# Norm tiles moved to another pool, a cross-attention head delayed by one unit, a quieter schedule in the second layer, and whole output rows at the end

## The chip, the core and the metric

The kernel is one program on one core of a Trainium2 chip. The metric is the time of one execution in microseconds (us) as the device measures it. Three timed executions of the kernel before took 946.2, 946.23 and 946.56 us, with a median of 946.23 us. A profiled execution of its own took 946.38 us.

The engines are named as in the profile: PE is TensorE (PEld its weight loads), DVE is VectorE, ACT is ScalarE, POOL is GpSimd and SP is SyncE, which here only issues DMAs.

## The reference

One step of a two-layer streaming encoder. There are 256 prompt frames and 32 sample frames (288 columns in all), 1024 features, 256 memory tokens and a feed-forward width of 2816. Cut to what matters:

```python
for layer in range(2):
    if layer == 0:   # 8 heads of chunk attention + 8 heads of stick-breaking attention
        x = x + merge_heads(chunk_attn(...), stick_break(...)) @ w_out_ab
    else:            # 16 heads of softmax attention with a forget bias
        q, k, v, log_f = proj_c(rmsnorm(x, g_mix), w_in_c, b_f)
        s = q @ k.T * 64 ** -0.5 + (cum_q - cum_k);  s = where(k_pos <= q_pos, s, -1e30)
        x = x + merge_heads(softmax(s) @ v) @ w_out_c
    mk, mv = memory_kv(mem, g_mem, w_xk, w_xv)               # 4 heads of 256
    x = x + (softmax(q4 @ mk.T / 16) @ mv) @ w_xo             # q4 = rmsnorm(x, g_xattn) @ w_xq
    x = x + (silu(h @ w_gate) * (h @ w_up)) @ w_down          # h = rmsnorm(x, g_ffn)
y = rmsnorm(x, g_final)                                        # rows are frames
```

`rmsnorm(x, g)` is `x * rsqrt(mean(x * x) + 1e-6) * g`. The keys and values are outputs too. All of it is float32.

## The kernel before

The residual `x` lies transposed in SBUF: eight blocks of 128 features by 288 columns. Every large product is done in a split form: an operand is cut into a rounded part (`hi`, `hh`, `oh`, `qh`) and the rest (`lo`, `hl`, `ol`, `ql`), and three matmuls (`mm3`, L193) add up to one product.

**Units.** The weights come in some 250 units. A unit is one 512 KB DMA of a 128x1024 tile `st` (issued by SP), a cast `hi` on ACT (L162), a subtraction `lo` on DVE (L163) and 24 matmuls into a PSUM bank. The tag `pj` has four banks; in the profile the matmuls are `pj` (projections and feed-forward), `op` (output projections), `mv` (memory values) and `dn` (down projection). All the small work, scores, transposes, softmax sums, uses another four banks of the tag `at` in turn, through the function `att`.

**What sets the order.** The small work of a head is a Python generator. `tick` (L239) runs after each unit and lets each active generator go one step; `wait(n)` (L232) makes a generator sit out n units. While `quiet` is set, `tick` only counts. `project(..., few=True)` sets `quiet` for one unit, so that small work piles up and is issued in one burst after a later unit. A scheduler orders the instructions inside such limits: how the program ends up on each engine is shown by the rows of the order below.

**Places of tiles.** `tok` (L49) gives one of 66 buffers of a common ring. `work` gives one of the eight `w` buffers that the attention uses. `bi`, `vn` (five each) and `w2` (four) are smaller sets.

**The norm.** `out_project` (L381) makes one block of `x` per unit and calls `nxt.block(m)`: ACT writes `hh` (L327), DVE `hl` (L330), ACT the square `sq` (L269), and POOL adds it to the running sum `ssq` (L282; the last of the eight additions runs on DVE). `begin` (L211) starts the next stage with two units, and after the first three steps of the second one calls `cur.scale()`. That leads to `wide` (L296), which splits the last `ssq` into `qh` (ACT, L403) and `ql` (DVE, L404) and multiplies both by a constant matrix (two `nrm` matmuls). Sites 2 and 3 are the norms between self-attention and cross-attention of the two layers, 6 and 7 the norms before the feed-forward, 8 the final one.

**Cross-attention** (L695). For each of four heads: two units of queries, then `head`: scores `xs`, softmax into `xe` (exponentials on ACT, the scaling on DVE at L443), `wait(1)`, four transposes `xt` (L731), a copy split in two, `wait(1)`, and the product `xo`. `room` (L705) chooses where the split queries lie. Sample frames run in pairs of heads as `xss`, `xst`, `xso` and `xsp`. Memory units (`mv` among them) are mixed in.

**Second layer's self-attention** (`mix_c`, from L1033). `proj(j, few)` runs three units (q, k, v) for each pair of heads, `attend(j)` the pair's prompt part: `sc` scores, `vt` transposed values, `tp` transposed weights, `po` product. `sample(g)` does the sample part (`ss`, `ts`, `os`, `ot`). `pairs` (L940) calls them in turn and passes `few` as true for all pairs but the first. Before, only the unit for k is quiet.

**The end.** The final norm gives one scale per frame, `y` turned into columns; PE turns `x` back into rows (`yt`), and ACT and DVE read the PSUM banks with the scale into `yo`, from which SP issues four DMAs. The last 32 frames (sample) lie in `strips`: 4 strips of 32 partitions by 256 columns in one bank.

Of the kernel before, what the change touches and what calls it, by code (L numbers as in the profile page):

```python
# [26 lines left out]
def encoder_step(ctx: ExitStack, tc: tile.TileContext, a):  # L27
# [17 lines left out]
    def name(s):  # L45
        cnt[0] += 1
        return f"{s}{cnt[0]}"
# [3 lines left out]

    def work(s):
        return wk.tile([P, 512], F32, tag="w", name=name(s))

    def work2(s, dt=F32):
        return wk.tile([P, 768], dt, tag="w2", bufs=4, name=name(s))
# [202 lines left out]
    class Norm:  # L259

        def __init__(self, n=NT, hurry=False):
            self.n, self.acc, self.parts, self.hurry = n, [None, None], 0, hurry
            self.tiles = [0, 128] + ([n - 128] if n > 256 else [])

        def add(self, xb, eng=None):
            q = tok("sq")
            S.activation(q[:, :self.n], xb[:, :self.n], AF.Square)  # L269
            self.parts += 1  # L270
            eng = eng or (V if self.parts == KT else G)
            i = int(self.parts == KT and self.hurry)
            if self.acc[i] is None:
                self.acc[i] = q
                return
            s = tok("ssq")
            b, c = self.acc[i][:, :self.n], q[:, :self.n]
            if self.parts == 2:

                V.scalar_tensor_tensor(s[:, :self.n], b, EPS * KT, c, op0=ALU.add, op1=ALU.add)  # L280
            else:
                eng.tensor_tensor(s[:, :self.n], b, c, ALU.add)  # L282
            self.acc[i] = s
# [11 lines left out]

        def wide(self):  # L296

            hi, lo = split(self.acc[0], tok("qh", F32R), tok("ql", F32R), V)
            p = att("nrm")[:, :self.n]
            mm(p, meanr, hi, True, False)  # L300
            mm(p, meanr, lo, False, True)
            r = big.tile([P, NT], F32, tag="rstd", bufs=2, name=name("rstd"))
            self.rsqrt(p, tok("y"), tok("nt"), r)
            return r

        def columns(self, between=None, bank=att):
# [26 lines left out]
    class Next:  # L333


        def __init__(self, gi):
            self.gi, self.norm, self.h, self.waiting = gi, Norm(hurry=gi == 8), ([], []), []

        def block(self, m, start=False):
            g = gain[:, self.gi * KT + m:self.gi * KT + m + 1]  # L340
# [282 lines left out]
    class Memory:  # L623
# [31 lines left out]
        def step(self):  # L655
            i, l = self.i, self.l
            self.i += 1
            if i < 8:
                p = project(a["w_xk"][l, i], self.h, NP)
                t = tok("mk")  # L660
                V.tensor_tensor(t[:, 0:NP], p[:, 0:NP], memrow, ALU.mult)
                store(a["mkT"][l, i], t[:, 0:NP])
                self.k.append(split(t[:, 0:NP], tok("kh", F32R)[:, 0:NP], tok("kl", F32R)[:, 0:NP]))
            else:

                i -= 8
                heads, n, u, last = (2, 2, i, 3) if i < 4 else (1, 4, i % 2, 1)
                if u == 0:
                    self.p = [acc("mv") for _ in range(heads)]
                w = unit(a["w_xv"][l, i])  # L670
                m = 256 * heads
                for c in range(n):
                    k = n * u + c
                    b = slice(c * m, c * m + m)
                    for t in range(2):
                        d, tb = self.p[t][:, 0:m] if heads == 2 else self.p[0][:, 256 * t:256 * t + 256], slice(128 * t, 128 * t + 128)
                        first = k == 0 and (heads == 2 or t == 0)
                        mm(d, self.h[0][k][:, tb], w[0][:, b], first, False)
                        mm(d, self.h[0][k][:, tb], w[1][:, b], False, False)
                        mm(d, self.h[1][k][:, tb], w[0][:, b], False, k == KT - 1)  # L680
                    if c == 1 and fine[0]:
                        tick(0.5)
                tick(0.5 if fine[0] else 1)
                if u == last:
                    for hd in range(heads):
                        for t in range(2):
                            d = self.p[t][:, 256 * hd:256 * hd + 256] if heads == 2 else self.p[0][:, 256 * t:256 * t + 256]
                            f = hd if heads == 2 else i // 2
                            v = tok("mv")
                            V.tensor_scalar(v[:, 0:NP], d, memcol[:, t:t + 1], None, op0=ALU.mult)  # L690
                            store(a["mv"][l, t, :, f * 256:f * 256 + 256], v[:, 0:NP])
                            self.v[t, f] = split(v[:, 0:NP], tok("vh", F32R)[:, 0:NP], tok("vl", F32R)[:, 0:NP], V if f == 3 else G)


    def cross(layer, cur, memory, nxt):  # L695
# [8 lines left out]

        def room(s, i):  # L705

            if i < 10:
                return wk.tile([P, NP], F32R, tag=("vn", "bi")[i % 2], bufs=5, name=name(s))
            if i % 2 == 0:
                room.pair = wk.tile([P, 2 * NP], F32R, tag="w2", bufs=4, name=name(s))  # L710
            return room.pair[:, (i % 2) * NP:(i % 2) * NP + NP]

        def evac(b, p):
            t = tok("xq")[:, 0:NP]
# [4 lines left out]
        def head(hd):  # L719
            yield 1  # L720
            s = att("xs")
            for t in range(2):
                for f in range(2):
                    mm3s(s[:, 256 * t:256 * t + 256], q[2 * hd + f], slice(128 * t, 128 * t + 128), memory.k[2 * hd + f], slice(0, NP), f == 0, f == 1)
            e = work("xe")
            softmax(s, [(0, 256), (256, 512)], None, e)
            yield from wait(1)
            tt = att("xt")
            for kt in range(2):
                for t in (1, 0):  # L730
                    i = T.transpose(tt[:, 256 * kt + 128 * t:256 * kt + 128 * t + 128], e[:, 256 * t + 128 * kt:256 * t + 128 * kt + 128], ident)  # L731
                    together(i)
            w = [wk.tile([P, 512], F32R, tag="w", name=name("xw")) for _ in range(2)]
            split_o(tt, w[0], w[1])
            yield from wait(1)
            po = att("xo")
            for f in range(2):
                for kt in range(2):
                    mm3s(po[:, 256 * f:256 * f + 256], memory.v[kt, hd], slice(128 * f, 128 * f + 128), w, slice(256 * kt, 256 * kt + 256), kt == 0, kt == 1)
            for f in range(2):  # L740
                split_o(po[:, 256 * f:256 * f + 256], o[0][2 * hd + f][:, 0:256], o[1][2 * hd + f][:, 0:256])
# [291 lines left out]
    def mix_c(cur, nxt, memory, w0):  # L1033
# [10 lines left out]
        def proj(j, few):  # L1044
            qs[j] = evac_q(cur, project(w[j], cur.h, begun=begun[0] if j == 0 else None))
            ks[j] = evac_kv(cur, project(w[8 + j], cur.h, begun=begun[1] if j == 0 else None, few=few), a["kv1"][j])
            vs[j] = evac_kv(cur, project(w[16 + j], cur.h), a["kv1"][8 + j])

        def attend(j):
            cp, sp, col = cum  # L1050
# [55 lines left out]
        cur = nxt  # L1106


    banks = [[acc("yt"), acc("yt")], [acc("yt"), acc("yt")]]
    strips = att("yt")  # L1110

    def turn(t, m):

        if t < 2:
            return T.transpose(banks[t][m // 4][:, P * (m % 4):P * (m % 4) + P], cur.h[0][m][:, P * t:P * t + P], ident)
        out = strips[NS * (m // 2):NS * (m // 2) + NS, P * (m % 2):P * (m % 2) + P]
        return mm(out, cur.h[0][m][:, P * t:NT], ident)

    def turn_early():
        for m in range(4):  # L1120
            turn(0, m)

    y = cur.norm.columns(turn_early)
    for t, m in [(2, m) for m in range(KT)] + [(0, m) for m in range(4, KT)] + [(1, m) for m in range(KT)]:
        not_before(turn(t, m), cur.norm.summed.ins)
    out = [wp.tile([P, 1024], F32, tag="st", bufs=4, name=name("yo")) for _ in range(3)]

    def read(eng, t, c0, c1):
        src, scale = (banks[t][c0 // 512] if t < 2 else strips), y[:, 2 * t:2 * t + 1]
        b = slice(c0 % 512, c0 % 512 + c1 - c0)  # L1130
        if eng is V:
            together(V.tensor_scalar(out[t][:, c0:c1], src[:, b], scale, None, op0=ALU.mult))
        else:
            together(S.activation(out[t][:, c0:c1], src[:, b], AF.Copy, scale=scale))


    read(V, 2, 0, 256)
    together(DMA.dma_start(a["y"][2 * P:NT].rearrange("q (s c) -> s q c", s=4), out[2][:, 0:256]))
    read(S, 0, 0, 256)
    read(V, 0, 256, 512)  # L1140
    together(DMA.dma_start(a["y"][0:P, 0:512], out[0][:, 0:512]))
    read(S, 0, 512, 768)
    read(V, 0, 768, 1024)
    together(DMA.dma_start(a["y"][0:P, 512:1024], out[0][:, 512:1024]))
    read(S, 1, 0, 512)
    read(V, 1, 512, 1024)
    together(DMA.dma_start(a["y"][P:2 * P], out[1]))


_OUTS = {  # L1150
# [80 lines left out]
```

## Time and profile before

| quantity | before |
|---|---|
| median of 3 timed runs | 946.23 us (946.2 to 946.56) |
| profiled execution | 946.38 us |
| its span (first to last instruction) | 944.7 us |
| PE busy | 930.4 us, 98% |
| DVE busy | 599.1 us, 63% |
| ACT busy | 485.9 us, 51% |
| POOL busy | 229.2 us, 24% |
| mean granted clock of TensorE | 0.999 of full speed |

The busy time of an engine is the time in which at least one of its instructions runs. A matmul takes longer than the distance to the next one, because they are pipelined, so distances between starts are what a PE step costs. In the waits view, a line gives an engine's instruction, what released it, the idle time in total, the count and the longest case. In a timeline, a row is: start, duration, engine, line, operation, tiles, count, and in brackets the idle time of the engine just before and what ended it.

### The profile page before, as it was taken

To read this page: it belongs to the slowest core of one execution; us is meant where nothing else is said; L and a number is where in the kernel's file an instruction comes from. 1 tells how busy PE (TensorE), PEld (TensorE's weight loads), DVE (VectorE), ACT (ScalarE), POOL (GpSimd) and SP (SyncE) were. 2 spreads that over 40 slices of the span, in tenths; PEclk is the share of its full clock that TensorE was granted. 3 is DMA by queue.
4 is the path that set the end of the run, shared out by engine and by line. 5 is a ranking of instruction groups with operands and counts; after the bars stand their busy time and mean duration, and the time that the engine had idled before them with its cause. 6 is when DMAs were issued, how large, how long until landed. Compare 5 with 4: busy or idle time off the path is not lost.

```text
span 944.7 us, 18787 instructions
## 1 busy us (share of the span) xinstructions
PE 930.4 (98%) x7350; PEld 899.2 (95%) x7350; DVE 599.1 (63%) x1145; ACT 485.9 (51%) x861; POOL 229.2 (24%) x347
## 2 busy tenths in 40 slices
PE   8999999999999999999999999999999999999996
PEld 8999999999999999999999999899999999999996
DVE  6795555886775555855486666668768655555442
ACT  6566876555554444444455555555546544444330
POOL 4341212201122222400026443322101322221010
PEclk9999999999999999999999999999999999999999
DMA  8675444553444544554556455444425544444431
GB/s 292 198 246 187 164 147 161 175 172 130 147 165 169 175 161 170 184 195 166 183 199 213 170 196 180 172 170 155 146 102 178 179 169 167 166 169 168 167 113 51
DMA packets 49629, 160.96 MB, mean 170 GB/s; under 512 B 7196, under 2 KB 8412, under 8 KB 49540
## 3 DMA queue, kind: packets, MB, share of 16 engines
q1 hardware_dynamic: 45348, 149.23, 46.3%
q0 software_dynamic: 3904, 10.04, 2.9%
q8 instruction: 58, 0.95, 0.4%
q10 hardware_dynamic: 288, 0.48, 0.2%
q14 instruction: 31, 0.25, 0.1%
HBM read 149.58 MB, written 10.15 MB: 169 GB/s over the span
## 4 chain that ended last, share of the span: by engine, by line
PE 95%; DVE 2%; ACT 1%; DMA 1%; issue 0%; POOL 0%; SPq 0%; DVEq 0%; ACTq 0%
PE pj L68 54%; PE dn L68 15%; PE op L68 10%; PE mv L68 5%; PE po L68 1%; PE sc L68 1%; PE zb L68 1%; PE xo L68 1%; PE xs L68 1%; DMA first<-w_first 1%; PE nrm L68 0%; PE xt L731 0%; PE xss L68 0%; PE os L68 0%; POOL ssq L282 0%
## 5 line engine op out<-in xcount | busy, mean ns | idle before, releaser
L162 ACT CAST hi<-st 128x1024 fp32r<-128x1024 f32 x257 | 268.9, 1050 | 287.7 <-issue 104.5
L68 PE MATMUL pj<-hh,hi 128*128 128x288 f32 (+1 forms) x1344 | 397.1, 295 | 0.0
L68 PE MATMUL pj<-hh,lo 128*128 128x288 f32 (+1 forms) x1344 | 394.1, 293 | 0.2 <-DVE lo L163 0.2
L68 PE MATMUL pj<-hl,hi 128*128 128x288 f32 (+1 forms) x1344 | 393.9, 293 | 0.0
L163 DVE TENSOR_TENSOR lo<-st,hi 128x1024 fp32r<-128x1024 f32 x257 | 316.0, 1230 | 80.2 <-PE dn L68 40.1
L68 PEld LDWEIGHTS pj<-hh,hi 128*128 128x128 f32 x1344 | 252.9, 188 | 5.3 <-issue 4.3
L68 PEld LDWEIGHTS pj<-hh,lo 128*128 128x128 f32 x1344 | 252.8, 188 | 0.6 <-DVE lo L163 0.6
L68 PEld LDWEIGHTS pj<-hl,hi 128*128 128x128 f32 x1344 | 252.9, 188 | 0.0
L68 PE MATMUL dn<-fh,hi 128*128 128x288 f32 x416 | 109.9, 294 | 0.0
L68 PE MATMUL dn<-fh,lo 128*128 128x288 f32 x352 | 103.4, 294 | 0.0
L68 PE MATMUL dn<-fl,hi 128*128 128x288 f32 x288 | 84.6, 294 | 0.0
L282 POOL TENSOR_TENSOR ssq<-ssq,sq 128x288 f32<-128x288 f32 (+1 forms) x35 | 37.3, 1066 | 185.7 <-ACT sq L269 151.1
L68 PE MATMUL op<-oh,hi 128*128 128x288 f32 x256 | 76.0, 298 | 0.0
L68 PE MATMUL op<-ol,hi 128*128 128x288 f32 x256 | 75.4, 295 | 0.0
L68 PE MATMUL op<-oh,lo 128*128 128x288 f32 x256 | 75.3, 295 | 0.0
L68 PEld LDWEIGHTS dn<-fh,hi 128*128 128x128 f32 x416 | 74.5, 188 | 0.0
L68 PEld LDWEIGHTS dn<-fh,lo 128*128 128x128 f32 x352 | 66.0, 188 | 0.0
L820 POOL TENSOR_TENSOR fl<-us,fh 128x288 fp32r<-128x288 f32 x36 | 33.2, 922 | 106.1 <-ACT fh L819 106.1
L816 POOL TENSOR_TENSOR gs<-gs,sg 128x288 f32<-128x288 f32 x44 | 39.3, 892 | 74.0 <-ACT sg L814 72.8
L815 DVE TENSOR_TENSOR us<-pj,rstd 128x288 f32<-128x288 f32 x44 | 20.1, 457 | 58.0 <-PE pj L68 58.0
L68 PEld LDWEIGHTS dn<-fl,hi 128*128 128x128 f32 x288 | 54.0, 188 | 0.0
L68 PEld LDWEIGHTS op<-oh,hi 128*128 128x128 f32 x256 | 47.9, 188 | 0.6
(282 smaller groups left out, 1215.8 us busy)
## 6 DMA issues: line engine op xcount, KB each, us to landing
st<-w_gate SPq DMA_DIRECT2D x44, 512.0 KB, 3.2
st<-w_up SPq DMA_DIRECT2D x44, 512.0 KB, 3.3
st<-w_down SPq DMA_DIRECT2D x44, 512.0 KB, 3.2
st<-w_c SPq DMA_DIRECT2D x24, 512.0 KB, 3.5
st<-w_ab SPq DMA_DIRECT2D x21, 512.0 KB, 4.3
st<-w_xk SPq DMA_DIRECT2D x16, 512.0 KB, 3.5
st<-w_xv SPq DMA_DIRECT2D x16, 512.0 KB, 3.3
st<-w_xq SPq DMA_DIRECT2D x16, 512.0 KB, 3.5
```

The source lines that it names most:

```text
L68: return T.matmul(out, lhsT, rhs, start=start, stop=stop, skip_group_check=True)
L162: a = S.copy(hi, st[:, c0:c1])
L163: b = V.tensor_tensor(lo, st[:, c0:c1], hi.bitcast(F32), ALU.subtract)
L282: eng.tensor_tensor(s[:, :self.n], b, c, ALU.add)
L815: V.tensor_tensor(us, pu[:, :NT], cur.r, ALU.mult)
L816: G.tensor_tensor(gs, gs, sg, ALU.mult)
L820: G.tensor_tensor(lo, us, hi.bitcast(F32), ALU.subtract)
```

## The change

It has four parts. First, `Norm` takes a function for its tiles, and at sites 2 and 3 that is `spare`, a `w` buffer (eight in all), in place of `tok`; the values of head 0 go to `bi` and the split queries to `w2` (three to a buffer) and `vn`. Second, the third cross head waits two units between its softmax and its `xt` transposes. Third, in the second layer's self-attention the unit for v is quiet too for j > 1. Fourth, the end reads and stores whole rows: frames 256 to 287 are transposed like the others into two banks of their own on 32 partitions, and each bank is read half by DVE and half by ACT.

```diff
+    def spare(s, dt=F32):
+        return wk.tile([P, NT], dt, tag="w", name=name(s))
...
-        def __init__(self, n=NT, hurry=False):
+        def __init__(self, n=NT, hurry=False, tile=tok):
...
-            q = tok("sq")
+            q = self.tile("sq")
...
-            s = tok("ssq")
+            s = self.tile("ssq")
...
-            hi, lo = split(self.acc[0], tok("qh", F32R), tok("ql", F32R), V)
+            hi, lo = split(self.acc[0], self.tile("qh", F32R), self.tile("ql", F32R), V)
...
-            self.gi, self.norm, ... = gi, Norm(hurry=gi == 8), ([], []), []
+            self.gi, self.norm, ... = gi, Norm(hurry=gi == 8, tile=spare if gi in (2, 3) else tok), ([], []), []
...
-                            self.v[t, f] = split(v[:, 0:NP], tok("vh", F32R)[:, 0:NP], tok("vl", F32R)[:, 0:NP], V if f == 3 else G)
+                            parts = [wk.tile([P, NP], F32R, tag="bi", bufs=5, name=name(s)) if f == 0 else tok(s, F32R)[:, 0:NP] for s in ("vh", "vl")]
+                            self.v[t, f] = split(v[:, 0:NP], *parts, V if f == 3 else G)
...
-            if i < 10:
-                return wk.tile([P, NP], F32R, tag=("vn", "bi")[i % 2], bufs=5, name=name(s))
-            if i % 2 == 0:
-                room.pair = wk.tile([P, 2 * NP], F32R, tag="w2", bufs=4, name=name(s))
-            return room.pair[:, (i % 2) * NP:(i % 2) * NP + NP]
+            if i > 11:
+                return wk.tile([P, NP], F32R, tag="vn", bufs=5, name=name(s))
+            if i % 3 == 0:
+                room.three = wk.tile([P, 3 * NP], F32R, tag="w2", bufs=4, name=name(s))
+            return room.three[:, (i % 3) * NP:(i % 3) * NP + NP]
...
-            yield from wait(1)
+            yield from wait(2 if hd == 2 else 1)
...
-            vs[j] = evac_kv(cur, project(w[16 + j], cur.h), a["kv1"][8 + j])
+            vs[j] = evac_kv(cur, project(w[16 + j], cur.h, few=few and j > 1), a["kv1"][8 + j])
...
-    read(V, 2, 0, 256)
-    together(DMA.dma_start(a["y"][2 * P:NT].rearrange("q (s c) -> s q c", s=4), out[2][:, 0:256]))
-    read(S, 0, 0, 256)
-    read(V, 0, 256, 512)
-    together(DMA.dma_start(a["y"][0:P, 0:512], out[0][:, 0:512]))
-    read(S, 0, 512, 768)
-    read(V, 0, 768, 1024)
-    together(DMA.dma_start(a["y"][0:P, 512:1024], out[0][:, 512:1024]))
-    read(S, 1, 0, 512)
-    read(V, 1, 512, 1024)
-    together(DMA.dma_start(a["y"][P:2 * P], out[1]))
+    for c in (0, 512):
+        read(V, 0, c, c + 256)
+        read(S, 0, c + 256, c + 512)
+        together(DMA.dma_start(a["y"][0:P, c:c + 512], out[0][:, c:c + 512]))
+    for t in (1, 2):
+        read(V, t, 0, 512)
+        read(S, t, 512, 1024)
+        together(DMA.dma_start(a["y"][P * t:min(P * t + P, NT)], out[t][rows[t]]))
```

ACT in the output projection before the first layer's cross-attention, blocks 3 to 6 of `x` (a row is line, operation, tile written, tiles read, shape; `hi` is the cast of a weight unit). Before:

```order
L162 CAST hi_2539<-st_2537 128x1024
L327 ACTIVATE hh_2310<-x_79,x_78 128x288
L269 ACTIVATE sq_2314<-x_79 128x288
L162 CAST hi_2608<-st_2606 128x1024
L162 CAST hi_2646<-st_2644 128x1024
L327 ACTIVATE hh_2350<-x_80,x_78 128x288
L269 ACTIVATE sq_2354<-x_80 128x288
L327 ACTIVATE hh_2390<-x_80,x_78 128x288
L269 ACTIVATE sq_2394<-x_80 128x288
```

The same blocks after:

```order
L165 CAST hi_2514<-st_2512 128x1024
L330 ACTIVATE hh_2310<-x_79,x_78 128x288
L272 ACTIVATE sq_2314<-x_79 128x288
L165 CAST hi_2539<-st_2537 128x1024
L330 ACTIVATE hh_2350<-x_80,x_78 128x288
L272 ACTIVATE sq_2354<-x_80 128x288
L165 CAST hi_2606<-st_2604 128x1024
L330 ACTIVATE hh_2390<-x_80,x_78 128x288
L272 ACTIVATE sq_2394<-x_80 128x288
```

Where two blocks and two casts stood in bunches, there is now one cast, one `hh` and one `sq` in turn. On PE the two `nrm` matmuls, which had three `pj` between them, now stand side by side, 27 `pj` after the start of the next stage as before.

PE in the first layer's cross-attention, around the `xt` of the third head (`pj` are the units of the queries of head 3, `mv` a memory unit). Before:

```order
L68 MATMUL pj_3001<-hl_2471,hi_2997 128x288
L68 MATMUL pj_3001<-hh_2470,lo_2998 128x288
L68 MATMUL pj_3047<-hh_2242,hi_3043 128x288
L68 MATMUL pj_3047<-hl_2243,hi_3043 128x288
L731 MATMUL xt_3026<-ident,xe_2972 128x128 x4
L68 MATMUL pj_3047<-hh_2242,lo_3044 128x288
L68 MATMUL pj_3047<-hh_2255,hi_3043 128x288
```

After:

```order
L71 MATMUL pj_3032<-hh_2470,hi_3028 128x288
L71 MATMUL pj_3032<-hl_2471,hi_3028 128x288
L71 MATMUL pj_3032<-hh_2470,lo_3029 128x288
L736 MATMUL xt_3057<-ident,xe_2965 128x128 x4
L71 MATMUL mv_3081<-hi_3084,hh_690 128x256
L71 MATMUL mv_3081<-lo_3085,hh_690 128x256
```

The transposes stood 26 `pj` behind the head's scores, and stand 48 behind them now. The later `xo` of this head moved behind the memory unit and the sample scores `xss`.

PE in the second layer's self-attention, at the end of a burst of small work (`ss` are scores of the sample part, `sc` those of the next pair of heads). Before:

```order
L465 MATMUL tp_6749<-ident,e_6643 128x128
L466 MATMUL tp_6749<-ident,e_6643 128x128
L68 MATMUL ss_6755<-ca_6652,q_6120 32x128
L68 MATMUL ss_6755<-kv_6128,q_6120 32x32
L68 MATMUL ss_6755<-ca_6652,q_6120 32x128
L68 MATMUL ss_6755<-kv_6128,q_6120 32x32
L68 MATMUL ss_6755<-ca_6652,q_6388 32x128
L68 MATMUL ss_6755<-kv_6421,q_6388 32x32
L68 MATMUL ss_6755<-ca_6652,q_6388 32x128
L68 MATMUL ss_6755<-kv_6421,q_6388 32x32
L68 MATMUL pj_6799<-hh_4961,hi_6795 128x256
L68 MATMUL pj_6799<-hl_4962,hi_6795 128x256
```

After:

```order
L470 MATMUL tp_6836<-ident,e_6638 128x128
L71 MATMUL ss_6842<-ca_6647,q_6115 32x128
L71 MATMUL ss_6842<-kv_6123,q_6115 32x32
L71 MATMUL ss_6842<-ca_6647,q_6115 32x128
L71 MATMUL ss_6842<-kv_6123,q_6115 32x32
L71 MATMUL ss_6842<-ca_6647,q_6383 32x128
L71 MATMUL ss_6842<-kv_6416,q_6383 32x32
L71 MATMUL ss_6842<-ca_6647,q_6383 32x128
L71 MATMUL ss_6842<-kv_6416,q_6383 32x32
L71 MATMUL sc_6857<-kv_6690,q_6657 128x128
L71 MATMUL sc_6857<-kv_6690,q_6657 128x256
L71 MATMUL sc_6869<-kv_6690,q_6657 128x128
```

Before, the burst ended here, 48 `pj` followed, then a second burst (`po`, `ts`, `sc`) and 48 more. After, the `sc` join the first burst, and 96 `pj` follow in one piece. Between the `sc` of the first pair and the first `mv` of this stage, there are twelve pieces of `pj` before; after, there are seven and a single matmul. In two of the merged bursts one `pj`, or two `mv`, stand between the `tp` of the two heads.

## Rows read from the trace of the kernel before

**Rows 1.** The page: PE's busy time, and the chain that ended last.

```profile
PE 930.4 (98%) x7350; PEld 899.2 (95%) x7350; DVE 599.1 (63%) x1145; ACT 485.9 (51%) x861; POOL 229.2 (24%) x347
PE 95%; DVE 2%; ACT 1%; DMA 1%; issue 0%; POOL 0%; SPq 0%; DVEq 0%; ACTq 0%
```

**Rows 2.** Waits of PE over the whole span: us, times, longest.

```profile
PE nrm L68 <- ACT qh L403: 2.5, 2, 1.2
PE xt L731 <- DVE xe L443: 1.9, 2, 1.0
PE pj L68 <- DVE lo L163: 0.2, 1, 0.2
```

**Rows 3.** Timeline of PE around the norm before cross-attention, both layers.

```profile
182.73 0.29 PE L68 MATMUL pj<-hl,hi 128*128 128x288 f32 x1
182.86 0.30 PE L68 MATMUL pj<-hh,lo 128*128 128x288 f32 x1
184.40 0.40 PE L68 MATMUL nrm<-qh,meanr 128*128 128x288 f32 x1 [1.24 <-ACT qh L403]
184.64 0.30 PE L68 MATMUL pj<-hh,hi 128*128 128x288 f32 x1
...
644.51 0.29 PE L68 MATMUL pj<-hh,lo 128*128 128x288 f32 x1
646.04 0.40 PE L68 MATMUL nrm<-qh,meanr 128*128 128x288 f32 x1 [1.25 <-ACT qh L403]
```

**Rows 4.** Timeline of POOL, DVE and ACT ahead of the first of them.

```profile
176.85 1.88 POOL L282 TENSOR_TENSOR ssq<-ssq,sq 128x288 f32<-128x288 f32 x1 [6.62 <-PE op L68]
...
183.44 0.45 DVE L282 TENSOR_TENSOR ssq<-ssq,sq 128x288 f32<-128x288 f32 x1
...
183.91 0.43 ACT L403 CAST qh<-ssq 128x288 fp32r<-128x288 f32 x1 [1.47 <-DVE ssq L282]
```

**Rows 5.** Timeline of the norm before the feed-forward, first layer: PE and ACT.

```profile
266.62 0.29 PE L68 MATMUL nrm<-qh,meanr 128*128 128x288 f32 x1
...
266.90 0.29 PE L68 MATMUL pj<-hh,hi 128*128 128x288 f32 x1
...
265.69 0.43 ACT L403 CAST qh<-ssq 128x288 fp32r<-128x288 f32 x1 [0.69 <-DVE ssq L282]
```

**Rows 6.** Timeline of PE and DVE at the third cross head, first layer.

```profile
219.86 0.29 PE L68 MATMUL pj<-hl,hi 128*128 128x288 f32 x1
221.14 0.63 PE L731 MATMUL xt<-ident,xe 128*128 128x128 f32 x4 [0.98 <-DVE xe L443]
...
219.42 1.57 DVE L443 TENSOR_SCALAR xe<-xe,st 128x256 f32<-128x256 f32 x2
```

**Rows 7.** Timeline of DVE and PE at the fourth cross head, first layer.

```profile
233.94 0.61 DVE L443 TENSOR_SCALAR xe<-xe,st 128x256 f32<-128x256 f32 x2
...
235.04 0.49 PE L731 MATMUL xt<-ident,xe 128*128 128x128 f32 x3
```

**Rows 8.** Timeline of PE, ACT and DVE in a burst of the second layer.

```profile
527.53 0.38 PE L68 MATMUL pj<-hh,hi 128*128 128x256 f32 x1
...
526.97 0.47 ACT L472 COPY pt<-tp 128x384 f32<-128x384 f32 x1
...
526.53 0.42 DVE L415 TENSOR_TENSOR ol<-po,oh 128x256 fp32r<-128x256 f32 x1
```

**Rows 9.** The page's group of all weight splits on DVE (count, us busy, mean ns).

```profile
L163 DVE TENSOR_TENSOR lo<-st,hi 128x1024 fp32r<-128x1024 f32 x257 | 316.0, 1230 | 80.2 <-PE dn L68 40.1
```

**Rows 10.** Timeline of SP, DVE and ACT at the end.

```profile
937.82 0.61 SPq L1138 DMA_DIRECT2D y<-yo  x1
...
939.53 0.51 SPq L1147 DMA_DIRECT2D y<-yo  x1
...
937.31 2.05 DVE L1132 TENSOR_SCALAR yo<-yt,y 128x256 f32<-128x256 f32 x4
...
937.32 1.42 ACT L1134 ACTIVATE yo<-yt,y 128x256 f32<-128x256 f32 x3 [2.57 <-DVE y L294]
```

More of the change, by code (lines that the diff above doesn't have):

```diff
@@ L259, in encoder_step @@
     class Norm:
-        def __init__(self, n=NT, hurry=False):
-            self.n, self.acc, self.parts, self.hurry = n, [None, None], 0, hurry
+        def __init__(self, n=NT, hurry=False, tile=tok):
+            self.n, self.acc, self.parts, self.hurry, self.tile = n, [None, None], 0, hurry, tile
             self.tiles = [0, 128] + ([n - 128] if n > 256 else [])
         def add(self, xb, eng=None):
-            q = tok("sq")
+            q = self.tile("sq")
             S.activation(q[:, :self.n], xb[:, :self.n], AF.Square)
@@ L302, in wide @@
             r = big.tile([P, NT], F32, tag="rstd", bufs=2, name=name("rstd"))
-            self.rsqrt(p, tok("y"), tok("nt"), r)
+            self.rsqrt(p, self.tile("y"), self.tile("nt"), r)
             return r
@@ L336, in __init__ @@
         def __init__(self, gi):
-            self.gi, self.norm, self.h, self.waiting = gi, Norm(hurry=gi == 8), ([], []), []
+            self.gi, self.norm, self.h, self.waiting = gi, Norm(hurry=gi == 8, tile=spare if gi in (2, 3) else tok), ([], []), []
         def block(self, m, start=False):
@@ L1106, in encoder_step @@
         cur = nxt
-    banks = [[acc("yt"), acc("yt")], [acc("yt"), acc("yt")]]
-    strips = att("yt")
+    banks = [[acc("yt"), acc("yt")], [acc("yt"), acc("yt")], [att("yt"), att("yt")]]
+    rows = [slice(0, P), slice(0, P), slice(0, NS)]
     def turn(t, m):
[L1114 to L1117, printed above, removed]
+        return T.transpose(banks[t][m // 4][rows[t], P * (m % 4):P * (m % 4) + P], cur.h[0][m][:, P * t:min(P * t + P, NT)], ident)
     def turn_early():
@@ L1123, in encoder_step @@
     y = cur.norm.columns(turn_early)
-    for t, m in [(2, m) for m in range(KT)] + [(0, m) for m in range(4, KT)] + [(1, m) for m in range(KT)]:
-        not_before(turn(t, m), cur.norm.summed.ins)
+    for t in range(3):
+        for m in range(4 if t == 0 else 0, KT):
+            not_before(turn(t, m), cur.norm.summed.ins)
     out = [wp.tile([P, 1024], F32, tag="st", bufs=4, name=name("yo")) for _ in range(3)]
     def read(eng, t, c0, c1):
-        src, scale = (banks[t][c0 // 512] if t < 2 else strips), y[:, 2 * t:2 * t + 1]
+        src, scale, r = banks[t][c0 // 512], y[rows[t], 2 * t:2 * t + 1], rows[t]
         b = slice(c0 % 512, c0 % 512 + c1 - c0)
         if eng is V:
-            together(V.tensor_scalar(out[t][:, c0:c1], src[:, b], scale, None, op0=ALU.mult))
+            together(V.tensor_scalar(out[t][r, c0:c1], src[r, b], scale, None, op0=ALU.mult))
         else:
-            together(S.activation(out[t][:, c0:c1], src[:, b], AF.Copy, scale=scale))
-    read(V, 2, 0, 256)
-    together(DMA.dma_start(a["y"][2 * P:NT].rearrange("q (s c) -> s q c", s=4), out[2][:, 0:256]))
-    read(S, 0, 0, 256)
-    read(V, 0, 256, 512)
-    together(DMA.dma_start(a["y"][0:P, 0:512], out[0][:, 0:512]))
-    read(S, 0, 512, 768)
-    read(V, 0, 768, 1024)
-    together(DMA.dma_start(a["y"][0:P, 512:1024], out[0][:, 512:1024]))
-    read(S, 1, 0, 512)
-    read(V, 1, 512, 1024)
-    together(DMA.dma_start(a["y"][P:2 * P], out[1]))
+            together(S.activation(out[t][r, c0:c1], src[r, b], AF.Copy, scale=scale))
+    for c in (0, 512):
[6 more added lines that the diff above has]
+        together(DMA.dma_start(a["y"][P * t:min(P * t + P, NT)], out[t][rows[t]]))
 _OUTS = {
```

## The prediction

> **What bounds the kernel now.** I read the page first: PE is busy in 98% of the span, and the chain that ended last runs over PE for 95% of its length [rows 1]. So a change in another engine counts only where PE stands still for it. Next the waits of PE. Leaving aside the start, where the change does nothing, there are three lines: 2.5 us for `nrm` behind the cast `qh`, 1.9 us for `xt` behind the softmax scaling `xe`, both in two places (one for each layer), and 0.2 us for a weight split [rows 2]. These 4.4 us are nearly all that can be had without removing matmuls. Then the timelines around these four places, which tell what each costs from one start on PE to the next, and what made the releaser late.
>
> **Norm tiles.** The last `pj` starts at 182.86 and `nrm` at 184.40, 1.54 us later; two `pj` in a row are 0.13 us apart (182.73 to 182.86). The stall is 1.41 us [rows 3]. In the second layer 644.51 to 646.04 gives 1.53 − 0.13 = 1.40 us [rows 3]. Why is `qh` late? It waited for the last `ssq` on DVE, and the row that explains this lies 7 us earlier: a POOL `ssq` began at 176.85 after 6.62 us of idleness that ended with an `op` matmul [rows 4]. An addition of squares has no use for an `op` matmul. What it waits for is its buffer: the common ring hands it one in which an attention output still lies, which the output projection reads to the end. After that all remaining squares and halves come in a bunch, POOL takes 1.88 us for one addition, and the end of the bunch is `ssq` at 183.44 and `qh` at 183.91 [rows 4].
>
> In buffers of its own set, the norm has nothing to wait for that the projection holds: the attention's `w` tiles are released before it starts. The order on ACT agrees, with one cast, one `hh` and one `sq` in turn. The nearest row of what it then does is the norm before the feed-forward: the same operations, the same 27 `pj` of cover, and tiles without pressure. There `qh` starts at 265.69 and ends at 266.12, and `nrm` goes at 266.62 without a wait, 0.50 us later [rows 5]. I take that site as the price: no stall. One more gain: two `nrm` in a row take 0.28 us to the next `pj` (266.62 to 266.90) [rows 5], while apart the first alone takes 0.24 us (184.40 to 184.64) and the second at least a pitch of 0.13 [rows 3], 0.37 together: 0.09 us for each site. Sum: −1.41 − 1.40 − 0.18 = −2.99 us. The bounds are the whole gain and, if the new places are held as well, nothing at all. The queries and the values of head 0 change places only to make room for this; they are written by the same instructions, none is added. I cost that at nothing, hidden by the `pj` of the following head.
>
> **Third cross head.** `xt` waits at 221.14 after a `pj` at 219.86: 1.28 − 0.13 = 1.15 us [rows 6]. The scaling `xe` took 1.57 us for two instructions there [rows 6], against 0.61 us for the same two in the fourth head [rows 7]. The idle time of PE is 0.98 us [rows 6] of 1.9 in both layers [rows 2], so the second layer's is 0.92, and with the same 0.17 between idle time and loss that is 1.09 us. With one unit more to wait, 48 `pj` stand between scores and `xt` in place of 26. The 22 more are 22 × 0.13 = 2.9 us, more than twice the stall, so even an `xe` that is as slow as now is in time, with 2.9 − 1.15 = 1.7 us to spare. Sum: −2.24 us.
>
> What is late next? `xo` of the same head still has a piece of 24 `mv` between it and `xt`, in place of 22 `pj`; equal cover. But its split `oh`, `ol` now falls on ACT and DVE right ahead of the fourth head's softmax. There the scaling ends at 234.55 and `xt` starts at 235.04 [rows 7]: 0.49 us of slack. The split has two `oh` and two `ol`; the nearest row has 0.42 us for one `ol` [rows 8]. If one of them comes in the way, the slack holds; if both do, 0.84 − 0.49 = 0.35 us is lost in each layer. I take 0, because the twelve matmuls of `xs` lie in between, and keep +0.7.
>
> **Second layer's bursts.** No matmul is added or removed. Six bursts become longer and pieces of `pj` fewer. A change of shape on PE costs about 0.11 us (a lone `nrm` 0.24 against 0.13 [rows 3]), so eight places fewer where `pj` resumes would give −0.9 us if the joints inside the burst were free. They aren't: `sc` behind `ss` is such a joint. I take 0 and keep −0.9 as the low end. The risk lies in four PSUM banks for all small work. In the burst of `po`, two `tp`, `ss`, the next `sc` takes the bank of `po`, and the one after it that of the first `tp`. Before, `pj` stood at that point, 527.53 [rows 8]. By then `ol` had read `po` (526.53 + 0.42 = 526.95), 0.58 us earlier. The copy `pt` ended at 527.44 [rows 8], 0.09 us earlier, but that bank is wanted by the second `sc` only, one pair of scores later. So by these rows nothing is waited for. The cover goes if a weight split `lo` gets ahead of `ol` on DVE: its mean is 1.23 us [rows 9], and `ol` would end some 0.5 us behind the start of `sc`. Behind the waiting `sc` all of PE stands. Six bursts at up to 0.5 us: +3 us is the high end, 0 what I take.
>
> **The end.** In the order before, ACT and DVE start at once on different banks (937.31 and 937.32), and the first DMA is issued at 937.82 after one read of the strips, the last, of 512 KB, at 939.53 [rows 10]. Now each bank is read by both, DVE first, and as both halves lie in one bank ACT's read stands behind DVE's. From the rows, three narrow and one wide read on DVE in 2.05 us, two narrow and one wide on ACT in 1.42 us: about 0.4 for a narrow and 0.7 for a wide one [rows 10]. DVE: 937.3, 937.7, 938.1, 938.8 to 939.5. ACT: 937.7, 938.1, 938.5, 939.2 to 939.9. The first issue is thus at 938.3, +0.5 us; the last at 939.95, +0.4 us, with 128 KB in place of 512 KB. The data are the same. Most of the span from the last issue to the end (944.7 − 939.53 = 5.2 us [rows 10]) is the way of a DMA, not its bytes. Between a full shift of +0.4 and a shorter last transfer I take +0.2; bounds −0.4 and +0.8.
>
> Here a rule of the Trainium skill speaks against the change: SBUF — State Buffer, section "Door 1: The DMA port swizzle (why `[64,N]` ≈ `[32,N]`)", says that the bandwidth of a DMA depends on how many of the 16 ports its partitions reach, and 32 partitions in a row reach eight. An estimate by that page's 27.2 GB/s for each port is 0.6 us for the last 128 KB in place of 0.3, so the sum would be +0.5 in place of +0.2 here. No row before shows a DMA of 32 partitions at the end.
>
> **Sum.** 946.38 (the profiled execution, span 944.7 and 1.7 around it) − 2.99 − 2.24 + 0 + 0.2 = 941.35. The profiled execution lies 0.15 us above the median of the timed runs, so I forecast 941.2 us.
>
> **The rivals.**
> - *The norm is still late.* The new set has eight buffers, shared with the cross head's `xe`; and POOL's additions may stay slow. Against it: the feed-forward site. If half of 1.4 us comes back in each layer, 942.6.
> - *The fourth head takes over the wait*, +0.7: 941.9. For it: 0.49 us of slack only. Against it: `xs` as cover.
> - *The bursts wait for PSUM banks*, up to 0.5 us in each of six: 942.7 to 944.2. For it: DVE has a `lo` near each burst, and four banks are few. Against it: 0.58 us of slack in the row.
> - *Slower.* The same mechanism with two steps of delay, `lo` ahead of `ol` and the softmax of the burst's first half ahead of both: 1.2 us or more in each of six bursts is +7.2, so 948.4. It decides from 0.85 us for a burst on (5.0 / 6). No row shows a wait of this kind now, and the slack speaks against it.
> - *The change doesn't do what it says:* then some `ssq` still waits for an `op` matmul, and 944.2 is left from the other parts.
>
> **How the numbers follow.** Forecast 66%, norm half late 11%, fourth head 10%, bursts 7%, slower 4%, norm unchanged 2%. The forecast's own range is 940.3 to 942.2, by the −0.9 of the joints and the ends of the tail. To leave out no more than 2 in 10, the range goes on to 943.8. A measurement tells 0.2%, 1.9 us, from no change: below 944.3 is faster. That holds for the forecast, the half-late norm, the fourth head and most of the bursts: 0.90. Same 0.06 and slower 0.04.
>
> **What would show it.** In the waits of PE, the lines `nrm` behind `qh` and `xt` behind `xe` are gone in both layers, and POOL's `ssq` has no idle time ended by `op`. The burst has `sc` behind `ss` with no idle time ahead of it; a line `sc` or `tp` behind `ol` or `pt` there would show the bank rival. At the end the first issue comes some 0.5 us after its old distance to the last `y`. I am wrong if PE's waits in the middle don't fall by about 4.4 us, or if they do and the span doesn't follow.

## The result and the profile after

The changed kernel took 940.01 us (median of 4 runs, 939.92 to 940.14), the kernel before 946.22 us (4 runs, 946.13 to 946.56). The ratio is 0.9934 (95% interval 0.9917 to 0.9951). That is 6.2 us less, where the prediction had 5.0 less; 940.01 lies 0.3 us below the low end of its range. The profiled execution took 940.14 us with a span of 938.3.

The page after, PE's busy time and the chain that ended last, which answer to [rows 1]:

```profile
PE 930.1 (99%) x7342; PEld 900.3 (96%) x7342; DVE 600.6 (64%) x1145; ACT 486.7 (52%) x862; POOL 232.2 (25%) x347
PE 99%; DVE 0%; POOL 0%; ACTq 0%; issue 0%; ACT 0%; POOLq 0%
```

PE's busy time is the same; the span is shorter. DVE's 2%, ACT's 1% and the 1% of the DMAs have gone from the chain. All waits of PE after, which answer to [rows 2]:

```profile
PE warm L143 <- POOL identb masks.py:199: 2.6, 1, 2.6
```

Only the start is left, which the change doesn't touch. The norm before the first cross-attention, PE, ACT and POOL after, in the places of [rows 3] and [rows 4]:

```profile
182.92 0.30 PE L71 MATMUL pj<-hh,lo 128*128 128x288 f32 x1
183.06 0.29 PE L71 MATMUL nrm<-qh,meanr 128*128 128x288 f32 x1
183.19 0.31 PE L71 MATMUL nrm<-ql,meanr 128*128 128x288 f32 x1
...
182.12 0.43 ACT L407 CAST qh<-ssq 128x288 fp32r<-128x288 f32 x1 [0.69 <-DVE ssq L285]
...
173.12 1.14 POOL L285 TENSOR_TENSOR ssq<-ssq,sq 128x288 f32<-128x288 f32 x1 [1.78 <-ACT sq L272]
175.43 0.99 POOL L285 TENSOR_TENSOR ssq<-ssq,sq 128x288 f32<-128x288 f32 x1 [1.18 <-ACT sq L272]
```

Here every `ssq` on POOL is now put down to its `sq` and none to an `op` matmul; in the second layer none is put down to `op` either. Such a line alone doesn't prove a wait for a buffer. At the norm before the feed-forward a `ssq` on POOL has it too, 2.33 us before (at 261.97) and 2.34 after (at 259.18), but before, the `sq` that it adds had ended only 0.13 us earlier, at 261.84. In [rows 4] the `sq` had ended at 171.85, 5.0 us ahead of the `ssq`, so the operand wasn't what was missing. `qh` ends at 182.55, 0.51 us ahead of `nrm`, as at the feed-forward site in [rows 5]. The third cross head, PE and DVE after, answering to [rows 6]:

```profile
221.30 0.60 PE L736 MATMUL xt<-ident,xe 128*128 128x128 f32 x4
...
217.75 1.60 DVE L447 TENSOR_SCALAR xe<-xe,st 128x256 f32<-128x256 f32 x2
```

`xe` is as slow as before (1.60 us), but ends at 219.35, 1.95 us ahead of `xt`. The fourth head, answering to [rows 7]:

```profile
231.33 0.62 DVE L447 TENSOR_SCALAR xe<-xe,st 128x256 f32<-128x256 f32 x2
...
232.26 0.60 PE L736 MATMUL xt<-ident,xe 128*128 128x128 f32 x4
```

Its slack shrank from 0.49 to 0.31 us and held. SP and the readers at the end, answering to [rows 10]:

```profile
933.11 0.82 SPq L1141 DMA_DIRECT2D y<-yo  x2
934.05 0.88 SPq L1145 DMA_DIRECT2D y<-yo  x2
...
932.00 2.18 DVE L1134 TENSOR_SCALAR yo<-yt,y 128x256 f32<-128x256 f32 x4
...
932.60 1.96 ACT L1136 ACTIVATE yo<-yt,y 128x256 f32<-128x256 f32 x4 [3.09 <-DVE yo L1134]
```

The first issue is 1.11 us behind the first read, against 0.51 before (937.31 to 937.82), and the last, the second of the two from 934.05 on, starts at 934.59 and is 2.59 behind it, against 2.22 (937.31 to 939.53); both as forecast. And yet from the first read to the end of the span it is 6.3 us (932.00 to 938.3), where it was 7.4 (937.31 to 944.7): from the last issue to the end 3.7 us in place of 5.2.

**Where the time went, by starts on PE.** The first `nrm` came 1.34 us earlier than before, the first `op` after the cross-attention 2.77 (234.66 against 231.89). The second layer's stage took 0.41 us back: from its first `sc` to its first `op` 108.00 us before (506.81 to 614.81) and 108.41 after (504.02 to 612.43). The first `yt` of the last stage then comes 5.23 us earlier (934.15 against 928.92), and 1.2 us are won behind it, at the end.

### The profile page after: what moved, and what is told of

Its sections match the earlier page's. It is cut to its first block, busy times and chain, and to the rows that moved or that the text cites. A ratio compares the mean times of both kernels' runs of the same rounds, so it can differ in the third digit from the quotient of the medians.

```text
span 938.3 us, 18754 instructions
## 1 busy us (share of the span) xinstructions
PE 930.1 (99%) x7342; PEld 900.3 (96%) x7342; DVE 600.6 (64%) x1145; ACT 486.7 (52%) x862; POOL 232.2 (25%) x347
## 4 chain that ended last, share of the span: by engine, by line
PE 99%; DVE 0%; POOL 0%; ACTq 0%; issue 0%; ACT 0%; POOLq 0%
PE pj L71 57%; PE dn L71 15%; PE op L71 11%; PE mv L71 5%; PE po L71 1%; PE xo L71 1%; PE xs L71 1%; PE sc L71 1%; PE zb L71 1%; PE xt L736 0%; PE xss L71 0%; PE os L71 0%; PE zs L71 0%; PE nrm L71 0%; PE warm L143 0%; PE vt L423 0%
```

## Experiments

All times are medians. Each group of kernels was timed beside the kernel before on its chip: 946.27 us for the first two groups, 946.37 for the last.

**The norm alone.** Part one of the diff as it stands, tiles and places.

```diff
+            self.gi, self.norm, ... = gi, Norm(hurry=gi == 8, tile=spare if gi in (2, 3) else tok), ...
+                            parts = [wk.tile([P, NP], F32R, tag="bi", ...) if f == 0 else tok(s, F32R)[:, 0:NP] for s in ("vh", "vl")]
+            if i > 11: ... tag="vn" ...   # queries: w2 (three to a buffer), then vn
```

> The norm's tiles and the places of the queries and of head 0's values alone, on the kernel before. Theory (the norm waited for a buffer of the output projection, and only that): both waits of PE for nrm are gone, -1.4 us for each layer and 0.1 for the two nrm side by side: 943.2 to 943.4 us. Rival (part of this gain needs the other parts, since the queries' new places also shorten the cross-attention): less than 2.5 us, 943.8 or more.

Measured: 942.83 us, ratio 0.9964 (0.9952 to 0.9977), −3.44 us. The theory holds, and 0.45 more than the prediction's 2.99 came. By starts on PE, less the 0.12 us by which this trace runs ahead from its start: `nrm` is 1.40 us earlier, the scores of the first head 1.50, of the second 1.65, the first `op` 1.73. So each layer gives 1.50 us as predicted and some 0.2 inside the cross-attention. Most of that comes between the first two heads, where `xt` of the first now stands right behind `xss` and four `pj` no longer come between.

**Tiles without places, and places without tiles.**

The first keeps `room` and the places of `vh` and `vl` as before, the second undoes one line of the kernel with the norm alone:

```diff
-            self.gi, self.norm, ... = gi, Norm(hurry=gi == 8, tile=spare if gi in (2, 3) else tok), ...
+            self.gi, self.norm, ... = gi, Norm(hurry=gi == 8), ...
```

> The norm's tiles in the w buffers, on the kernel before, with the queries and head 0's values in their old places. Theory (the ring of 66 was the bottleneck for the norm's own tiles): the waits of PE for nrm are gone, 943.4 us; the 0.3 to 0.4 us beyond the norm's stall that the whole part gave belongs to the places. Rival (the halves hh and hl still wait in the ring: two sq stand ahead of their hh on ACT): part of the wait remains, 944.3 to 945.5.

> The queries and head 0's values in their new places, on the kernel before, with the norm's tiles in the common ring as before. Theory of the prediction (the places only make room, they gain nothing): 946.2 us, or 945.9 with the small gains inside the cross-attention. Rival (head 0's values held ring buffers, and freeing these alone lets the norm's chain run on time): 943 to 944.5.

Measured: 942.91 us (ratio 0.9964, 0.9951 to 0.9976) and 942.85 (0.9963, 0.9949 to 0.9976). Each half alone gives the whole gain. That the places only make room is wrong: freeing ring buffers in another way does the same as taking the norm out of the ring. By the code only head 0's values leave the ring with the places, four tiles in each layer; the queries were never in it. The 0.2 us inside the cross-attention come with either half, so they don't belong to the places alone, which I had expected: in both runs `xt` of the first head stands right behind `xss`. With the places alone, one `ssq` on POOL does still wait for an `op` matmul, for a shorter time:

```profile
176.99 1.88 POOL L285 TENSOR_TENSOR ssq<-ssq,sq 128x288 f32<-128x288 f32 x1 [2.72 <-PE op L71]
179.42 0.81 POOL L285 TENSOR_TENSOR ssq<-ssq,sq 128x288 f32<-128x288 f32 x1 [0.56 <-ACT sq L272]
```

Against [rows 4] the idle time is 2.72 us in place of 6.62, and no second bunch follows. That what decides is how many buffers the ring is short of, and not which tile is moved, fits both runs. No run counts the buffers, so it isn't shown.

**The third head alone.**

```diff
-            yield from wait(1)
+            yield from wait(2 if hd == 2 else 1)
```

> The third cross head a unit later, alone, on the kernel before. Theory (PE loses the idle time before xt, and the layout around it has fewer changes of shape): -1.15 and -1.09 by the prediction, 944.0 us; by the starts of the changed kernel up to 0.2 us more in each layer, 943.6. Rival (the wait moves to the fourth head, whose softmax now stands behind a split): 0.7 us of it come back, 944.7.

Measured: 943.93 us, ratio 0.9975 (0.9965 to 0.9985), −2.34 us. PE's wait for `xe` is gone from both layers and no other line took its place. The rival fell.

**The quiet v unit alone.**

```diff
+            vs[j] = evac_kv(cur, project(w[16 + j], cur.h, few=few and j > 1), ...)
```

> The quiet v unit of the second layer alone, on the kernel before. The prediction took 0. Theory from the starts of the changed kernel (614.81 - 506.81 before, 612.43 - 504.02 after): the stage is 0.41 us longer, 946.6 us. Rival (that 0.4 us belongs to the tiles' new places, which the stage shares): no change, 946.2.

Measured: 946.80 us, ratio 1.0005 (0.9997 to 1.0014), so from this ratio alone a cost isn't certain; but all 11 runs (946.61 to 946.92) lie above the median of before, and by starts the stage takes 108.41 us (506.73 to 615.14), the same 0.41 more as in the changed kernel. Where it sits is seen in the changed kernel's PE, in the burst at 572:

```profile
572.13 0.27 PE L470 MATMUL tp<-ident,e 128*128 128x128 f32 x1
572.15 0.38 PE L71 MATMUL pj<-hh,hi 128*128 128x288 f32 x1
572.37 0.28 PE L468 MATMUL tp<-ident,e 128*128 128x128 f32 x1
...
572.80 1.18 PE L71 MATMUL sc<-kv,q 64*128 64x128 f32 x8
573.90 0.40 PE L71 MATMUL pj<-hl,hi 128*128 128x288 f32 x1
```

The eight `sc` of a burst take 0.86 us to the next start in every burst before, and after for instance from 530.77 to 531.63. Here they take 1.10, and in the burst at 546 they take 0.92. That makes 0.24 and 0.05 of the 0.41 us. The other 0.11 is the balance of all other distances between starts in the stage. The large matmuls lie in 15 pieces before (12 of `pj`, 3 of `mv`) and in 13 after (8 and 5), so two returns are saved, and the new joints inside the bursts cost a little more than that. One of them is the single `pj` between the `tp`, with 0.22 to the next start in place of a pitch of 0.13. That the `sc` at 572 wait for DVE's copy of `ts`, which ends at 572.74, fits the order of the banks, but the profile names no wait, and it wasn't tried.

**The changed kernel without that part.**

> The changed kernel without the quiet v unit. If that part costs what the starts of the changed kernel say (0.41 us in the second layer's self-attention), 939.6 us, ahead of the changed kernel. If the part costs nothing: 940.0.

Measured: 939.62 us, ratio 0.9928 (0.9916 to 0.9941). Without the part the changed kernel is 0.4 us faster: all 5 runs (939.37 to 939.65) lie below its 4 (939.92 to 940.14), though the intervals of the two ratios overlap.

**Whole rows at the end alone.**

> Whole rows at the end alone, on the kernel before. Theory one (the strided store of the strips stood at the head of the queue and held up all behind it): -1.2 us, 945.0. Theory two (the prediction's: a later first and last issue, shorter last transfer): +0.2, 946.4.

Measured: 945.27 us, ratio 0.9989 (0.998 to 0.9998), −1.0 us. The prediction's theory falls. The rate of the DMAs shows why. In the four rows of rates that follow here and below, each number is one fortieth of a window. First the kernel before (938.8 to 943.8, 0.125 us a number), then the changed kernel (933.6 to 938.3, 0.12 us):

```profile
GB/s 0 0 41 41 25 16 74 115 131 131 164 238 360 426 393 377 418 426 426 410 426 475 410 393 426 442 459 426 360 426 393 164 131 66 98 131 0 0 0 0
```

```profile
GB/s 0 0 17 349 366 471 366 471 331 453 366 418 401 418 523 418 453 349 488 453 383 418 418 453 349 314 383 209 0 0 0 0 0 0 0 0 0 0 0 0
```

Before, the stores crawl for about 1.2 us, run at some 400 GB/s, and then five numbers trail at 66 to 164. After, they run at full rate from the second number above zero to the last but one. The data are the same 1.18 MB. In the packet records of the kernel before, 4 to 6 pieces of 1 KB and 12 or 13 of 2 KB are under way at once at 940.35, 940.5 and 940.65. From 942.9 to 943.2 just four are, of 4 KB, as if the part that carried the strips came out last; the records don't name the engine.

**The strips' store last, and left out.** In the second, the last 32 rows of y are not written.

```diff
-    together(DMA.dma_start(a["y"][2 * P:NT].rearrange("q (s c) -> s q c", s=4), out[2][:, 0:256]))
...
     together(DMA.dma_start(a["y"][P:2 * P], out[1]))
+    together(DMA.dma_start(a["y"][2 * P:NT].rearrange("q (s c) -> s q c", s=4), out[2][:, 0:256]))   # first kernel only
```

> The kernel before with the store of the strips (128 pieces of 1 KB) issued last, all reads in place. Theory one (this store is slow to get going and holds up what is queued behind it): with nothing behind it the 2 KB pieces start in a body on all 16 engines, as in the changed kernel, some 1 us earlier in their course; the strips' own slow start is then at the end, which gives back up to as much: 945.2 to 946.2 us. Theory two (the last transfer's size sets the end): the last one is 128 KB, 945.2 or less, but also if the stores before it start as slowly as now.

> The kernel before without the store of the strips: the last 32 rows of y are not written. Theory one: 1.0 to 1.3 us less, 944.9 to 945.2 us, and the first 2 KB pieces run at full rate. Theory two (only bytes count; 128 KB of 1.18 MB at the rate of the trace is 0.3 us): 945.9.

Measured: 947.16 us with the store last (ratio 1.0008, 0.9999 to 1.0017) and 944.80 without it (0.9984, 0.9975 to 0.9993). So 128 KB of 1.18 MB are worth 1.5 us at the head of the queue and 2.4 at its tail. Here the theory had the right culprit, and my expectation for the store last was too low: nothing covers it there. Its rates, 939 to 945, 0.15 us a number:

```profile
GB/s 0 287 396 355 410 396 423 423 437 437 424 410 382 437 437 437 437 437 62 21 14 0 0 14 7 20 75 82 96 102 96 102 89 89 27 7 0 0 0 0
```

The three plain stores are nearly through by 941.7. Then for 1.2 us little moves, and at last the strips go at about 90 GB/s, a quarter of the rate or less. In the packet records of this trace the 128 pieces of 1 KB take 2.6 us (941.74 to 944.33), half of that time four at once, and hardly ever more than five.

**The same pieces in a plain store.**

```diff
+        for d in ((c, c + 256) if c == 0 else (c,)):
+            w = 256 if c == 0 else 512
+            together(DMA.dma_start(a["y"][0:P, d:d + w], out[0][:, d:d + w]))   # in the kernel with whole rows
```

> Whole rows at the end alone, on the kernel before, but the first store cut in two plain ones of 128 partitions by 256 columns (1 KB pieces, without the strips' rearrangement). Theory one (the rearranged store runs on 5 of 16 engines; 1 KB pieces as such do no harm): the 1 KB pieces lie on all 16 engines, and the time is within 0.4 us of the kernel with whole rows alone, 945.3 to 945.7 us. Rival (1 KB pieces are the slow thing): 25 or so pieces of some 90 ns on few engines, or a late end, 946.3 or more.

Measured: 945.60 us (ratio 0.9992, 0.9983 to 1.0001), 0.3 us above the kernel with whole rows alone. Here 256 pieces of 1 KB went in 1.07 us, some 20 under way at once at most. Small pieces are not the cause; the rearranged pattern is. Its outermost dimension is 4, and four at once is what is seen, not the five that I expected. The Trainium skill has the rule (DMA: Bandwidth & Descriptors, "Why a DMA increments its semaphore by 16 and not by 1"): the number of engines is the largest up to 16 that divides the slowest dimension of both sides, so 4 here, and 16 for 32 or 128 rows. These traces agree. The packet counts of the two windows above, before and after, tell the same:

```profile
DMA packets 564, 1.18 MB, mean 236 GB/s; under 512 B 52, under 2 KB 180, under 8 KB 564
```

```profile
DMA packets 480, 1.18 MB, mean 251 GB/s; under 512 B 64, under 2 KB 64, under 8 KB 480
```

The packets under 512 B have 4 bytes each. There are 48 of them for three plain stores (the run without the strips' store), 52 with the strips' store, 64 for four plain stores and 80 for five (this run). So each plain store has 16, of 32 rows as of 128, and the strips' store has 4. No run gave the strips' store another outermost dimension and left all else alone; that the number of engines is the cause rests on these counts.

**Rows in place of strips, in the old order.** Two reads of 32 partitions, that store first, the rest as before.

```diff
+    read(V, 2, 0, 512)
+    read(S, 2, 512, 1024)
+    together(DMA.dma_start(a["y"][2 * P:NT], out[2][0:NS]))
     read(S, 0, 0, 256)
     ...                     # as before, the 512 KB store last
```

> The kernel before with the last 32 frames as rows (two banks, a store of 32 pieces of 4 KB), but in the old order: that store first, the 512 KB store last, and other reads as before. Theory one (pattern of the strips): -0.8 to -1.2 us, 945.0 to 945.4. Theory two (the order and the size of the last store): no gain, 946.2. Rule of the pages on 32 partitions: the head of the queue is held up by eight ports, 0.3 us later than theory one.

Measured: 945.36 us (ratio 0.999, 0.9981 to 0.9998), the same as whole rows alone within 0.1 us. So the order and size of the stores don't show in the time; that the strips are gone does. The rates, 938.8 to 942.8, 0.1 us a number:

```profile
GB/s 164 328 164 164 328 164 0 0 143 307 410 389 430 410 369 410 430 410 348 430 451 553 369 533 410 369 492 328 410 410 369 492 451 328 41 0 0 0 0 0
```

The 32-partition store runs alone in the first six numbers, at 219 GB/s on their mean. The Trainium skill (SBUF — State Buffer, "Door 1") gives eight ports at 27.2 GB/s, 218 GB/s: the rule that the prediction weighed holds. It costs nothing measurable here, at the head (945.36 us) or as the last store (945.27). At the head nothing is kept waiting: the two zeros behind the six numbers show that the next store had not begun when this one was through.

**The best of them.** The changed kernel without the quiet v unit, the first 128 rows read as two wide reads at the same time.

```diff
-    for c in (0, 512):
-        read(V, 0, c, c + 256)
-        read(S, 0, c + 256, c + 512)
+    for eng, c in ((V, 0), (S, 512)):
+        read(eng, 0, c, c + 512)
```

> The changed kernel without the quiet v unit, and with the first 128 rows read as two wide reads at the same time (DVE columns 0 to 511, ACT columns 512 to 1023) in place of a DVE and an ACT read of each bank after one another. Theory (the stores run at full rate from their start, so the end follows the first issue): a read of 0.74 us in place of 0.4 + 0.2 + 0.4, the first issue some 0.25 us earlier, and so the end: 939.4 us. Rival (the last issue sets the end, it hardly moves): 939.6.

Measured: 939.20 us (939.11 to 939.40), ratio 0.9925 (0.9912 to 0.9937): faster than the kernel before, and 0.8 us faster than the changed one, 0.4 of which is the quiet v unit. From the first read to the first issue it takes 0.78 us (931.44 to 932.22) in place of 1.09 without the wide reads (931.31 to 932.40).

## Why the prediction was wrong

- **What bounds the kernel**: right in the main. Four waits of PE were most of what there was, and all four are gone. They were not nearly all: the end, where PE has done its work, gave 1.0 us more.
- **Norm tiles**: right in place, mechanism and price of the stall (1.40 us and 0.10 in each layer against 1.41 and 0.09). Mis-sized by 0.45 us, since I counted nothing inside the cross-attention. Wrong in the small step that the places only make room: they alone do the whole.
- **Third cross head**: right, 2.34 us against 2.24, and the fourth head did not take it over.
- **Second layer's bursts**: I took 0; it is 0.41 to 0.53 us. 0.29 of it lies in the `sc` of two of the three bursts with both a `ts` and an `sc`. `ts` takes a bank of its own, and I had worked out the slack from a burst without one; that the bank is the cause is not shown. The low end of −0.9 us was wrong too: it counts eight places fewer where `pj` resumes, but the pieces of `pj` fall from 12 to 8, and those of `mv` rise from 3 to 5. At 0.11 us for each that is −0.2 to −0.4.
- **The end**: this is the step that failed. I forecast +0.2 us with −0.4 as the lower bound; it measured −1.0 alone and about −1.2 within the whole. The issue times came out as forecast. What was wrong is the sentence that most of the span from the last issue to the end is "the way of a DMA, not its bytes": these 5.2 us became 3.7, with the same bytes. In the span before, the strips' store ran four pieces at once and held up the stores behind it. I priced the stores by their issues and bytes and not by the rate of the DMAs over those 5 us, where the crawl stood in the trace of before.
- **The sum**: −3.44 − 2.34 + 0.53 − 1.0 = −6.25, and the whole change measured −6.2. The parts add up, so nothing was lost between them. The range was missed for want of a low bound at the end. Its low end was the −0.9 us of the bursts alone, without the end's own lower bound. With both, 941.2 − 0.9 − 0.6 = 939.7 would have held the measurement, but by luck, since neither term has that size.

## What to carry to other kernels

Read the DMA rates over the tail in narrow slices before pricing a store by its bytes, and give a store an outermost dimension of a multiple of 16: whole rows in place of an outermost 4 gave 1.0 us here. When a small chain is released by an unrelated matmul and its own operands have long been there, look for a buffer that it waits for. Here two ways of relieving the ring gave the same, and both at once no more than one. Before merging bursts of small matmuls, count the returns to the large ones that are really saved: here two, and the new joints gave them back.

## What the runs showed of the hardware beyond that

A slow store holds up those behind it on the same queue: with the strips at its head, 2 KB pieces that need 1.4 us in the changed kernel (933.95 to 935.39) were spread over 2.6 (939.59 to 942.19). Two `xe` scalings took 1.6 us in the third head and 0.6 in the fourth, before and after alike. In the trace of before the first of the two in the third head starts at 219.42 and takes 0.35 us, like each of those in the other heads; the second starts at 219.69 and takes 1.30, to 220.99. During it POOL issues a store (`mv`, 219.51 for 0.56 us) and works on a split (`vl`, 220.09 to 220.83), and it ends 0.16 us behind that split. It is so in both layers and in both kernels (1.28 to 1.33 us), and POOL does nothing during the `xe` of the other heads. So the `xe` that PE waited for may have been held up by POOL; no run moved POOL's work, and that isn't shown.
